# Seven block products in place of eight for the first products of two feed-forward blocks

## The chip, the cores and the metric

The kernel runs on one core of a Trainium2 chip. The metric is device time in microseconds, the median of several runs. TensorE (PE) multiplies, VectorE (DVE) and ScalarE (ACT) do element-wise work, GpSimd (POOL) does a little of it, and SyncE (SP) issues the transfers (DMA) that bring weights from memory. Each engine takes its instructions in the order in which they were written to it.

## What is computed

Two transformer blocks follow each other on 1024 tokens of 1024 features; only their feed-forward parts are touched. Block 1 has 2816 inner features (22 tiles of 128), block 2 has 4096 (32 tiles).

```python
# block 1
h = rms_norm(x, g_ffn) * (1.0 + sc_f) + sh_f
x = x + g_f * ((silu(h @ w_ffn_gate) * (h @ w_ffn_up)) @ w_ffn_down)
# block 2
h = rmsnorm(x, norm_mlp_g)
x = x + square(relu(h @ w_up)) @ w_down
```

## The kernel before

Activations are kept transposed, features on the 128 partitions: x is 8 feature tiles (k) by two token halves (t) of 512 columns. Each fp32 operand is split into a high and a low part: ACT casts the high one, DVE or POOL subtracts it for the low one (`split`, `weights`). Each 128x128 by 128x512 product is then three matmuls: high by high (L253), low activation (L254), low weight (L255). Names ending in h and l are these parts: hh and hl of the normalised input, uh and ul of the inner activation, wh and wl of the weights.

`ffn` (L1144) runs in chunks of inner tiles. For a chunk it first makes the first products (`up`, 8 k-tiles each, gate and up in block 1, up alone in block 2), evacuates each from its PSUM bank (sg is silu of the gate; re is relu, then squared), and splits it into uh and ul (`u_split`). Then come the second products (`down`): for each of 8 output tiles and both token halves the chunk's inner tiles are summed in a bank and added to x by DVE (L100 in block 1, L97 in block 2). Block 1's chunks are 2, 4, 4, 4, 4, 4 inner tiles, block 2's are eight chunks of 4. In a down chunk a group is two output tiles, the first token half ahead of the second; so the last u of a chunk (inner tile 3, second half) is wanted by the 34th matmul of the group, behind 33 others.

PE's order is that of the code. Work that was put off (`later`, `tick`) is written between matmuls: the normalised input of the second token half (`make_h`) is made while the first half is multiplied. Weights are fetched by SP into wr (two buffers of 512 KB), each transfer issued when the buffer's last reader is done. SP also writes x out for a later use (`spill`, x1d). In the last chunk of block 1 `evac_last` also sums the squares of x twice, once on DVE and once on POOL (acc, through buffers ta, four of them).

Of the kernel before, what the change touches and what calls it, by code (L numbers as in the profile page):

```python
# [5 lines left out]
F32 = mybir.dt.float32  # L6
F32R = mybir.dt.float32r
# [6 lines left out]
P = 128  # L14
# [9 lines left out]
HOLD = 1  # L24


TAGS = {
    "g": (32, 512),
    "pt": (6, 512),
    "h": (32, 512),  # L30
    "wr": (2, 1024),
    "wh": (2, 1024),
    "wl": (2, 1024),
    "e": (7, 1024),
    "td": (4, 512),
    "ta": (4, 512),
}


def rev(ap, n):  # L40
# [10 lines left out]
class Build:  # L51
    def __init__(self, tc, a, out, dbg=None):
        self.tc, self.nc, self.a, self.out = tc, tc.nc, a, out
        self.dbg = dbg or {}
        self.n = 0
        self.bg = None
        self.due = {"d": [], "s": []}
        self.dense, self.b, self.ready = None, 0.0, set()
        self.pend = []
        self.pre, self.pace = [], 1  # L60
        self.low = self.nc.gpsimd
        self.fresh = set()
        self.quarter = None


    def nm(self, s):
# [1 line left out]
        return f"{s}_{self.n}"  # L68

    def al(self, tag, dt=F32, cols=None, name=None):  # L70
        bufs, w = TAGS[tag]
        return self.sb.tile([P, cols or min(w, 1024)], dt, name=self.nm(name or tag), tag=tag, bufs=bufs)

    def small(self, cols, tag, bufs=2, dt=F32):
        return self.sb.tile([P, cols], dt, name=self.nm(tag), tag=tag, bufs=bufs)
# [251 lines left out]
        self.nc.scalar.copy(r, ps)  # L327
        return r

    def rstd_then(self, acc, n, eps, then, gap=3):  # L330
        d = self.rtok([acc], n, eps)[0]
        self.later(gap, lambda: then(self.spread(d)))


    def consts(self):
# [748 lines left out]
    def block1_mix(self):  # L1084
        self.gdo = self.const(1, "gdo")
        self.ts(self.gdo, self.v("g_diff_out"), 1.0 - LAM_INIT, ALU.mult)
        self.dn = self.const(64, "dn")
        self.dnd = self.dram([32, P], "dnd")
        self.alibi()
        self.modd = self.dram([4, 2, H], "modd")  # L1090
        self.bg = self.mod_later()
        self.xd = self.spill("xd", 2)
        od = [[self.dram([P, H], "od") for _ in range(2)] for _ in range(8)]
        self.D = {}
        t3, tl = self.t_gemm(24), self.t_gemm(48)
# [36 lines left out]
        def evac2(n, t, ps):  # L1132
            evac(n, t, ps)
            self.sq_acc(accs, t, self.x[n][t])
        self.hh, self.hl = self.h_tiles()

        def done(t):
            def then(r):
                for k in range(KT):
                    self.later(1 + (2 - t) * k, lambda k=k: self.make_h(self.hh, self.hl, k, t, r, A[:, k : k + 1], sh[:, k : k + 1]))  # L1140
            self.rstd_then(accs[t], T, self.eps1, then)
        self.drain(self.gemm(W, 512, 4, cols, hh, hl, evac2, done, gsz=8))

    def ffn(self, chunks, up, down, evac_down, evac_last, done, gsz, cut=False):  # L1144

        c0 = 0
        for ci, c in enumerate(chunks):
            uh, ul = [[None, None] for _ in range(c)], [[None, None] for _ in range(c)]
            self.drain(up(c0, c, uh, ul))
            last = ci == len(chunks) - 1  # L1150
            self.drain(self.gemm(down, c0 * P, c, [[(i * P, P)] for i in range(8)], uh, ul,
                                 evac_last if last else evac_down, done if last else None, gsz=gsz if last else 2, cut=cut))
            c0 += c

    def u_split(self, tmp, uh, ul, i, t):
        tag = "g" if i < 3 else "pt"
        uh[i][t], ul[i][t] = self.al(tag, F32R, name="uh"), self.al(tag, F32R, name="ul")
        self.split(tmp, uh[i][t], ul[i][t])

    def block1_ffn(self):  # L1160
        Wg, Wu = self.a["w_ffn_gate"][0], self.a["w_ffn_up"][0]

        def up(c0, c, uh, ul):
            nt = []
            for i in range(c):
                nt += [(Wg, [((c0 + i) * P, P)]), (Wu, [((c0 + i) * P, P)])]
            hold = {}

            def evac(n, t, ps):
                if n % 2 == 0:  # L1170
                    hold[t] = self.al("td", name="sg")
                    self.act(hold[t], ps, AF.Silu)
                else:
                    s = hold[t]
                    self.tt(s, ps, s, ALU.mult)
                    self.u_split(s, uh, ul, n // 2, t)
            return self.gemm(None, 0, KT, nt, self.hh, self.hl, evac, gsz=2)
        g = self.mod[:, 40:48]
        gf = self.v("g_final", 0, 8)
        gg = self.const(8, "gg")  # L1180
# [6 lines left out]
        def evac_last(n, t, ps):  # L1187
            evac(n, t, ps)
            self.sq_acc(a1, t, self.x[n][t])
            self.sq_acc(a2, t, self.x[n][t], scale=gf[:, n : n + 1], tag="e", eng=self.nc.gpsimd if n < KT - 1 else None)  # L1190
        hh, hl = self.h_tiles()

        self.r1 = self.const(8, "r1")
# [1 line left out]
        def done(t):  # L1195
# [13 lines left out]
            d = v[:, 4:8]  # L1209

            def then():
                r = self.spread(d)
# [339 lines left out]
    def block2_mix(self):  # L1552
# [72 lines left out]
            self.sq_acc(accs, t, self.x[n][t])  # L1625
        self.hh, self.hl = self.h_tiles()

        def done(t):
            def then(r):
                for k in range(KT):  # L1630
                    self.later(1 + (2 - t) * k, lambda k=k: self.make_h(self.hh, self.hl, k, t, r, self.v("norm_mlp_g_2", k), tag="gh"[t]))
            self.rstd_then(accs[t], T, self.eps2, then)
        self.drain(self.gemm(W, 0, KT, cols, hh, hl, evac2, done, gsz=2))

    def block2_ffn(self):
        Wu = self.a["w_up_2"][0]

        def up(c0, c, uh, ul):
            def evac(n, t, ps):
                s = self.al("td", name="re")  # L1640
                self.act(s, ps, AF.Relu)
                self.tt(s, s, s, ALU.mult)
                self.u_split(s, uh, ul, n, t)
            return self.gemm(Wu, 0, KT, [[((c0 + i) * P, P)] for i in range(c)], self.hh, self.hl, evac, gsz=2)
        accs = {}

        def evac(n, t, ps):
# [21 lines left out]
        def done(t, s):  # L1669
# [29 lines left out]
                elif hf:  # L1699
                    self.nc.sync.dma_start(out=d, in_=o)  # L1700
            for i in range(n):
                o = self.al("e", name="out")
# [14 lines left out]
    def run(self, upto=99):  # L1717
        tc = self.tc
        with tc.tile_pool(name="sb", bufs=1) as self.sb, tc.tile_pool(name="ps", bufs=1, space=PSUM) as self.ps, \
                tc.tile_pool(name="dp", bufs=1, space=DRAM) as self.dp:  # L1720
            with tc.manual_schedule(engines={mybir.EngineType.PE}):
                self.phases(upto)

    def phases(self, upto):
        self.block1_in()
# [51 lines left out]
```

## Time and profile before

| what | us |
|---|---|
| median of 3 runs | 3242.78 (3242.65 to 3246.18) |
| profiled execution | 3245.43 |
| its span | 3243.5 |
| PE busy in it | 3109.9 (96%) |
| DVE, ACT, POOL busy | 1792.0, 1250.5, 428.1 |
| block 1 feed-forward, first matmul to last | 655.3 to 1400.5 |
| block 2 feed-forward, first matmul to last output | 2513.2 to 3243.5 |

A matmul of 512 columns is shown with about 0.4 us but the next one starts 0.23 us later: they overlap, so the pace is read from starts. A gap in the starts with "[idle <- engine tile]" is time in which PE waited for that tile.

### The profile page before, as it was taken

What the parts mean: (1) busy time and instruction counts of PE and PEld (TensorE: products, weight loads), DVE (VectorE), ACT (ScalarE), POOL (GpSimd) and SP (SyncE); (2) the same over time, 40 slices, a digit from 0 to 9 for tenths busy, and PEclk for the clock granted to TensorE, in tenths of its full rate; (3) what the DMA queues carried; (4) which work ended last, traced back from release to release, by engine and by line L of the source; (5) the groups of instructions that cost most, each with busy time, mean ns of one, the idle gap of its engine ahead of it and who ended that gap; (6) DMA issues with size and microseconds to landing.
All of it is one profiled execution on the core that took longest, in us unless ns stands there. A gap on an engine that the chain in (4) does not pass through costs nothing. (4 is left out here: it accounts for less than half of the span.)

```text
span 3243.5 us, 39354 instructions
## 1 busy us (share of the span) xinstructions
PE 3109.9 (96%) x15270; PEld 2528.2 (78%) x15270; DVE 1792.0 (55%) x2999; ACT 1250.5 (39%) x2220; POOL 428.1 (13%) x431
## 2 busy tenths in 40 slices
PE   6899999999999999989999998999999999999999
PEld 4777778878888888868777776877788788888888
DVE  5666677552322323367777779778973533333335
ACT  4444576331111111355665664555532322211215
POOL 3101111110000000043332332111112100000000
PEclk8999999999999999999999999999999999999999
DMA  8434304111111111232222221222531111111111
GB/s 266 111 94 115 100 24 146 40 39 46 52 46 46 52 43 48 81 82 62 66 64 60 54 56 34 85 74 77 172 95 46 46 46 46 52 46 46 52 46 72
DMA packets 265036, 229.37 MB, mean 71 GB/s; under 512 B 16908, under 2 KB 221562, under 8 KB 264850
## 3 DMA queue, kind: packets, MB, share of 16 engines
q1 hardware_dynamic: 257408, 214.14, 22.8%
q10 hardware_dynamic: 7090, 12.65, 1.0%
q8 instruction: 120, 1.97, 0.3%
q14 instruction: 66, 0.54, 0.1%
q0 software_dynamic: 352, 0.07, 0.0%
HBM read 176.91 MB, written 24.74 MB: 62 GB/s over the span
## 5 line engine op out<-in xcount | busy, mean ns | idle before, releaser
L253 PE MATMUL mm<-hh,wh 128*128 128x512 f32 (+1 forms) x2208 | 887.3, 402 | 12.3 <-ACT wh L201 7.5
L255 PE MATMUL mm<-hh,wl 128*128 128x512 f32 (+1 forms) x2208 | 879.4, 398 | 1.3 <-POOL wl L202 1.2
L254 PE MATMUL mm<-hl,wh 128*128 128x512 f32 (+1 forms) x2208 | 873.4, 396 | 2.5 <-DVE hl L97 2.4
L201 ACT CAST wh<-wr 128x1024 fp32r<-128x1024 f32 (+3 forms) x231 | 231.2, 1001 | 810.7 <-PE mm L254 657.6
L253 PEld LDWEIGHTS mm<-hh,wh 128*128 128x128 f32 (+1 forms) x2208 | 415.5, 188 | 103.8 <-ACT wh L201 7.7
L255 PEld LDWEIGHTS mm<-hh,wl 128*128 128x128 f32 (+1 forms) x2208 | 414.8, 188 | 103.6 <-POOL wl L202 2.5
L254 PEld LDWEIGHTS mm<-hl,wh 128*128 128x128 f32 (+1 forms) x2208 | 415.3, 188 | 94.6 <-DVE hl L97 3.0
L202 POOL TENSOR_TENSOR wl<-wr,wh 128x1024 fp32r<-128x1024 f32 (+3 forms) x105 | 234.5, 2235 | 1046.2 <-ACT wh L201 962.4
L254 PE MATMUL mm<-ul,wh 128*128 128x512 f32 (+1 forms) x816 | 316.7, 388 | 0.0
L253 PE MATMUL mm<-uh,wh 128*128 128x512 f32 (+1 forms) x816 | 316.4, 388 | 0.0
L255 PE MATMUL mm<-uh,wl 128*128 128x512 f32 (+1 forms) x816 | 316.0, 387 | 0.0
L202 DVE TENSOR_TENSOR wl<-wr,wh 128x1024 fp32r<-128x1024 f32 (+1 forms) x126 | 152.3, 1208 | 207.3 <-ACT wh L201 202.6
L97 DVE TENSOR_TENSOR x<-x,mm 128x512 f32<-128x512 f32 (+1 forms) x168 | 111.0, 661 | 239.0 <-PE mm L255 238.1
L1285 DVE TENSOR_TENSOR_SCAN u<-u 128x128 f32<-128x128 f32 (+7 forms) x128 | 177.8, 1389 | 76.6 <-POOL u L1281 76.1
L253 PEld LDWEIGHTS mm<-uh,wh 128*128 128x128 f32 x816 | 153.3, 188 | 33.2
L254 PEld LDWEIGHTS mm<-ul,wh 128*128 128x128 f32 x816 | 153.2, 188 | 32.9
L255 PEld LDWEIGHTS mm<-uh,wl 128*128 128x128 f32 x816 | 153.1, 188 | 32.2
L97 DVE TENSOR_TENSOR sg<-mm,sg 128x512 f32<-128x512 f32 x43 | 29.7, 691 | 258.2 <-PE mm L255 258.2
L100 DVE SCALAR_TENSOR_TENSOR x<-mm,mod,x 128x512 f32<-128x512 f32 x128 | 95.5, 748 | 132.4 <-PE mm L255 131.9
L108 ACT ACTIVATE u<-sc 128x512 f32<-128x512 f32 (+2 forms) x192 | 95.0, 495 | 96.2 <-PE sc L1273 94.6
L108 ACT ACTIVATE p<-p,mx 128x128 f32<-128x128 f32 (+7 forms) x96 | 74.6, 778 | 105.0 <-DVE mx L97 67.5
L97 DVE TENSOR_TENSOR al<-tp,ah 128x512 fp32r<-128x512 f32 (+1 forms) x160 | 99.3, 621 | 23.1 <-ACT ah L112 22.9
(392 smaller groups left out, 5037.2 us busy)
## 6 DMA issues: line engine op xcount, KB each, us to landing
wr<-in_w_in SPq DMA_DIRECT2D x65, 512.0 KB
wada<-in_w_ada SPq DMA_DIRECT2D x48, 512.0 KB
wr<-in_w_up SPq DMA_DIRECT2D x32, 512.0 KB
wr<-in_w_down SPq DMA_DIRECT2D x32, 512.0 KB
wr<-in_w_out SPq DMA_DIRECT2D x24, 512.0 KB
wr<-in_w_ffn_gate SPq DMA_DIRECT2D x22, 512.0 KB
wr<-in_w_ffn_up SPq DMA_DIRECT2D x22, 512.0 KB
wr<-in_w_ffn_down SPq DMA_DIRECT2D x20, 512.0 KB
```

Source lines behind the costliest of these rows:

```text
L97: return self.nc.vector.tensor_tensor(o, i0, i1, op)
L100: return self.nc.vector.scalar_tensor_tensor(o, i0, s, i1, op0, op1)
L108: return self.nc.scalar.activation(o, i, f, **k)
L201: self.nc.scalar.copy(wh[:, :n], raw[:, :n])
L202: (low or self.low).tensor_tensor(wl[:, :n], raw[:, :n], wh[:, :n].bitcast(F32), ALU.subtract)
L253: mm(o, lhsT=wh[:, k, :], rhs=xh[k][t][:, s], start=(k == 0), stop=False)
L254: mm(o, lhsT=wh[:, k, :], rhs=xl[k][t][:, s], start=False, stop=False)
L255: mm(o, lhsT=wl[:, k, :], rhs=xh[k][t][:, s], start=False, stop=(k == KC - 1))
L1285: nc.vector.tensor_tensor_scan(ur, ur, ur, 1.0, ALU.mult, ALU.bypass)
```

## The change

The first products of every chunk but the first are made in groups (`pair_weights`, `pair_job`) of two output tiles by two token halves, with the eight k-tiles in two halves of four: a 2x2 by 2x2 block product with seven block products (P1 to P7) in place of eight. Each block product is 4 k-tiles of three matmuls, 12 in all. In block 1 a group is the gate and the up of one inner tile (20 groups), in block 2 two inner tiles (15 groups). The sums of activation blocks (T: P5, P6, P7, P4) are made once at each feed-forward's start by `make_t` (y0, t2, t3, t4, split into th and tl); the sums of weight blocks are made by DVE for each group (P6, P7, P3; buffers ws). Every block product has its own 128x512 weight split in a buffer wc, of which there are four; the two halves of a chunk's down weights take two 128x1024 wc each. Three banks collect: U (P1, P6, P7, P4), A (P2), V (P5, P3); ACT copies a partial sum out (c), DVE adds them, and `fin` does the silu or relu and the split.

Chunks are two inner tiles (11 in block 1, 16 in block 2). Down tiles run first half, second half, output tile by output tile, 6 matmuls each. Chunk 0 is made plainly (`first_chunk`). Job i's fetch is written seven jobs ahead and its weights two jobs ahead. Buffers are laid out anew (`layout`): MIX outside, FFN inside the feed-forward parts, with four wr, four wc, eight u and two ta.

```diff
+ORDER = ("P1", "P2", "P6", "P5", "P7", "P3", "P4")
+BANK = {"P1": "U", "P2": "A", "P6": "U", "P5": "V", "P7": "U", "P3": "V", "P4": "U"}
+FFN = {"td": (4, 512), "ta": (2, 512), "wr": (4, 1024), "ws": (2, 1024), "wc": (4, 1024), "u": (8, 512), "hx": (8, 512)}
...
+        def sums(k):
+            q = k + 4
+            y0 = self.al("td", name="y0")
+            self.stt(y0, self.x[k][0], col(A, k), r[0], ALU.mult, ALU.mult)
+            t2 = self.al("td", name="t2")
+            self.tt(y0, y[k], y0, ALU.subtract)
+            plus(t2, y[q], sh is None or col(sh, q), y0)
+            pair("P5", k, y0)
...
+        self.t_work = [lambda k=k: sums(k) for k in range(4)] + [lambda k=k: last(k) for k in range(4)]
+        for k in range(early):
+            self.later(9 + 2 * k, lambda: self.t_work.pop(0)())
...
+        def make(p):
+            if p == "P6":
+                s = self.al("ws")
+                st["s"] = (s[:, :H], s[:, H:])
+                self.tt(st["s"][0], side(1, 0), side(1, 1), ALU.add)
+                self.tt(st["s"][1], st["s"][0], side(0, 0), ALU.subtract)
+            elif p == "P7":
+                self.tt(side(1, 0), side(0, 0), side(1, 0), ALU.subtract)
+            elif p == "P3":
+                self.tt(st["s"][1], side(0, 1), st["s"][1], ALU.subtract)
...
+            w = self.al("wc", F32R)
+            self.split(src, w[:, :H], w[:, H:])
...
+        for k, (xh, xl) in enumerate(self.moving(p)):
+
+            mm(o, lhsT=wh[:, k, :], rhs=xh, start=(new and k == 0), stop=False, skip_group_check=True)
+            mm(o, lhsT=wh[:, k, :], rhs=xl, start=False, stop=False, skip_group_check=True)
+            mm(o, lhsT=wl[:, k, :], rhs=xh, start=False, stop=(k == 3), skip_group_check=True)
+            self.tick()
+        if p in ("P1", "P6", "P5"):
+            st["c" + p] = self.al("td", name="c")
+            self.nc.scalar.copy(st["c" + p], o)
+        elif p == "P2":
+            self.tt(st["cP1"], o, st["cP1"], ALU.add)
+            fin(0, 0, st["cP1"])
...
+        else:
+            fin(1, 0, o)
...
+        def make():
+            hi, lo = self.al("wc", F32R), self.al("wc", F32R)
+            self.split(st["raw"], hi, lo)
...
+                        for n in range(4 * g, 4 * g + 4):
+                            for t in range(2):
+                                self.down_tile(st, n, t, (), uh, ul, evac_down)
...
+        self.first_chunk([s for two in pairs(0) for s in two], plain(0))
+        self.flush()
+        while self.t_work:
+            self.t_work.pop(0)()
+        fetched = made = 0
+        for i in range(len(jobs)):
+            while fetched < min(len(jobs), i + 8):
+                if jobs[fetched][0]:
+                    jobs[fetched][0]()
+                fetched += 1
+            while made < min(len(jobs), i + 3):
+                jobs[made][1]()
+                made += 1
+            jobs[i][2]()
...
-        self.ffn([2, 4, 4, 4, 4, 4], up, self.a["w_ffn_down"][0], evac, evac_last, done, 8)
+        self.ffn(11, pairs, plain, fin, self.a["w_ffn_down"][0], evac, evac_last, done)
+        self.layout(MIX)
...
-        self.ffn([4] * 8, up, self.a["w_down_2"][0], evac, evac_last, done, 8, cut=True)
+        self.ffn(16, pairs, plain, fin, self.a["w_down_2"][0], evac, evac_last, done, cut=True)
```

DVE at the end of a chunk's first products in block 1, before (sg and ul of the last two inner activations, wl the low parts of the coming down weights, x the first down tile's evacuation):

```order
L97 TENSOR_TENSOR ul_8058<-sg_8029,uh_8057 128x512
L202 TENSOR_TENSOR wl_8121<-wr_8118,wh_8120 128x1024
L97 TENSOR_TENSOR sg_8086<-mm_8088,sg_8086 128x512
L202 TENSOR_TENSOR wl_8183<-wr_8180,wh_8182 128x1024
L97 TENSOR_TENSOR ul_8115<-sg_8086,uh_8114 128x512
L100 SCALAR_TENSOR_TENSOR x_5341<-mm_8124,mod,x_5341 128x512
```

The same place after the change (c_8428 the second token half's silu and product, wc_8489 the low part of the down weights' second half, c_8386 the product of P4's bank mm_8373, ul_8506 its split, x_5344 the first down tile's evacuation):

```order
L106 TENSOR_TENSOR wr_8410<-wr_8408,wr_8410 128x512
L106 TENSOR_TENSOR c_8428<-tp_8434,c_8428 128x512
L106 TENSOR_TENSOR c_8428<-c_8447,c_8428 128x512
L106 TENSOR_TENSOR wc_8489<-wr_8388,wc_8488 128x1024
L106 TENSOR_TENSOR ul_8485<-c_8428,uh_8484 128x512
L106 TENSOR_TENSOR c_8386<-mm_8373,c_8386 128x512
L106 TENSOR_TENSOR ul_8506<-c_8386,uh_8505 128x512
L109 SCALAR_TENSOR_TENSOR x_5344<-mm_8512,mod,x_5344 128x512
```

The 128x1024 low part, which stood among evacuations that had a chunk's matmuls before their use, now stands between the last two activations; its buffer is the one that P4's weights leave, and the product of P4 and its split stand behind it.

DVE at the first down chunk of block 2, before (re and ul are inner activations, wl the low part of a weight, x_19951 the first down tile's evacuation):

```order
L97 TENSOR_TENSOR re_21740<-re_21740 128x512
L97 TENSOR_TENSOR ul_21744<-re_21740,uh_21743 128x512
L202 TENSOR_TENSOR wl_21814<-wr_21811,wh_21813 128x1024
L97 TENSOR_TENSOR re_21772<-re_21772 128x512
L97 TENSOR_TENSOR ul_21776<-re_21772,uh_21775 128x512
L202 TENSOR_TENSOR wl_21876<-wr_21873,wh_21875 128x1024
L97 TENSOR_TENSOR re_21804<-re_21804 128x512
L97 TENSOR_TENSOR x_19951<-x_19951,mm_21817 128x512
```

The same place after (y, t and tl are sums of `make_t` and their low parts, wc_22301 and wc_22305 the low parts of the first down weights):

```order
L106 TENSOR_TENSOR tl_22261<-y_4714_22255,th_22260 128x512
L106 TENSOR_TENSOR t_4697_22162<-t_4697_22162,t_4715_22257 128x512
L106 TENSOR_TENSOR tl_22267<-t_4715_22257,th_22266 128x512
L106 TENSOR_TENSOR t_4720_22270<-y_22082,y_22073 128x512
L106 TENSOR_TENSOR tl_22281<-t_4675_22100,th_22280 128x512
L106 TENSOR_TENSOR wc_22301<-wr_22292,wc_22300 128x1024
L106 TENSOR_TENSOR tl_22273<-t_4720_22270,th_22272 128x512
L106 TENSOR_TENSOR tl_22285<-t_4697_22162,th_22284 128x512
L106 TENSOR_TENSOR wc_22305<-wr_22294,wc_22304 128x1024
L106 TENSOR_TENSOR tl_22289<-t_4697_22162,th_22288 128x512
L106 TENSOR_TENSOR x_20462<-x_20462,mm_22311 128x512
```

The sums of `make_t` now stand in DVE's row ahead of the first down weights' low part and of the first evacuation.

SP at the end of block 1, before (x1d are spills, in_w_in the weights of block 2's first product):

```order
L194 DMA wr_10392<-in_w_ffn_down 128x4x256
L194 DMA wr_10867<-in_w_in 128x8x128
L515 DMA x1d_10787<-x_5341 128x512
L515 DMA x1d_10789<-x_5343 128x512
L194 DMA wr_10873<-in_w_in 128x8x128
L515 DMA x1d_10791<-x_5345 128x512
```

The same place after:

```order
L524 DMA x1d_11277<-x_5368 128x512
L524 DMA x1d_11279<-x_5370 128x512
L524 DMA x1d_11281<-x_5372 128x512
L524 DMA x1d_11283<-x_5374 128x512
L203 DMA wr_11348<-in_w_in 128x8x128
L203 DMA wr_11354<-in_w_in 128x8x128
L203 DMA wr_11602<-in_w_in 128x8x128
```

The first two weight transfers, which stood ahead of and among the spills, now stand behind all sixteen.

## Rows read from the trace of the kernel before

**Rows 1.** The page, busy time by engine, then TensorE and its clock by slice.

```profile
PE 3109.9 (96%) x15270; PEld 2528.2 (78%) x15270; DVE 1792.0 (55%) x2999; ACT 1250.5 (39%) x2220; POOL 428.1 (13%) x431
...
PE   6899999999999999989999998999999999999999
...
PEclk8999999999999999999999999999999999999999
```

**Rows 2.** Busy time by stretch: window, length, PE, PEld, DVE, ACT, POOL, clock, DMA.

```profile
655.30:704.90 49.60, 47.74 (x209) 37.65 (x210) 22.35 (x29) 19.57 (x32) 7.52 (x6) 1.00 0.05 17
...
816.30:860.30 44.00, 44.00 (x194) 35.96 (x193) 17.45 (x21) 4.72 (x6) 0.00 (x0) 1.00 0.16 48
860.30:950.00 89.70, 89.70 (x386) 72.17 (x385) 19.97 (x23) 17.02 (x24) 0.00 (x0) 1.00 0.16 47
...
2513.20:2543.40 30.20, 26.21 (x114) 19.28 (x113) 25.83 (x30) 14.69 (x26) 15.26 (x9) 1.00 0.07 21
...
2565.50:2609.70 44.20, 44.20 (x195) 36.12 (x194) 16.47 (x22) 5.44 (x7) 0.00 (x0) 1.00 0.17 48
2609.70:2654.10 44.40, 44.40 (x194) 36.20 (x193) 14.96 (x19) 12.57 (x19) 0.00 (x0) 1.00 0.15 48
...
3183.60:3243.50 59.90, 54.15 (x369) 49.48 (x367) 33.34 (x61) 35.60 (x64) 0.00 (x0) 0.97 0.21 80
```

**Rows 3.** Timeline of PE at the end of a block 1 down chunk: start, length, instruction.

```profile
993.70 0.40 PE L255 MATMUL mm<-uh,wl 128*128 128x512 f32 x1
993.93 0.40 PE L253 MATMUL mm<-hh,wh 128*128 128x512 f32 x1
```

**Rows 4.** DVE instructions by line, block 1, 860.3 to 1350: count, busy, mean ns.

```profile
L202 DVE TENSOR_TENSOR wl<-wr,wh 128x1024 fp32r<-128x1024 f32 x44 | 53.9, 1226 | 73.2 <-ACT wh L201 69.9
L100 DVE SCALAR_TENSOR_TENSOR x<-mm,mod,x 128x512 f32<-128x512 f32 x49 | 36.8, 750 | 80.3 <-PE mm L255 80.1
L97 DVE TENSOR_TENSOR sg<-mm,sg 128x512 f32<-128x512 f32 x31 | 21.4, 692 | 192.5 <-PE mm L255 192.5
L97 DVE TENSOR_TENSOR ul<-sg,uh 128x512 fp32r<-128x512 f32 x31 | 21.3, 688 | 11.0 <-ACT uh L112 11.0
```

**Rows 5.** ACT instructions by line, same stretch.

```profile
L112 ACT CAST uh<-sg 128x512 fp32r<-128x512 f32 x31 | 19.2, 621 | 92.7 <-DVE sg L97 92.7
```

**Rows 6.** Timeline of PE at two idle gaps and behind them.

```profile
1403.27 0.47 PE L253 MATMUL mm<-hh,wh 128*128 128x512 f32 x1 [2.77 <-DVE x L100]
...
1404.05 0.63 PE L253 MATMUL mm<-hh,wh 128*128 128x512 f32 x1
1404.48 0.63 PE L254 MATMUL mm<-hl,wh 128*128 128x512 f32 x1
...
2517.89 0.50 PE L254 MATMUL mm<-hl,wh 128*128 128x512 f32 x1 [2.36 <-DVE hl L97]
2518.23 0.39 PE L255 MATMUL mm<-hh,wl 128*128 128x512 f32 x1
2518.46 0.40 PE L253 MATMUL mm<-hh,wh 128*128 128x512 f32 x1
```

**Rows 7.** Timeline of DVE, first rows of the second token half, block 2.

```profile
2525.77 2.08 DVE L100 SCALAR_TENSOR_TENSOR xn<-x,vec,r 128x512 f32<-128x512 f32 x3 [1.29 <-ACT r L327]
```

**Rows 8.** Timeline of SP around block 1's end: weight and spill issues.

```profile
1355.33 0.37 SPq L194 DMA_DIRECT2D wr<-in_w_in  x1
1356.60 1.19 SPq L515 DMA_DIRECT2D x1d<-x  x2
1359.51 0.38 SPq L194 DMA_DIRECT2D wr<-in_w_in  x1
```

**Rows 9.** SP: a gate weight issued ahead of block 1's feed-forward.

```profile
641.20 0.37 SPq L194 DMA_DIRECT2D wr<-in_w_ffn_gate  x1
```

**Rows 10.** POOL and ACT by line in block 1's last chunk, 1350.9 to 1400.5.

```profile
L302 POOL TENSOR_TENSOR acc<-acc,sq 128x512 f32<-128x512 f32 x10 | 14.0, 1402 | 691.7 <-ACT sq L108 690.2 <-DVE acc L302 1.5
...
L108 ACT ACTIVATE sq<-x,vec 128x512 f32<-128x512 f32 x11 | 7.8, 712 | 0.0
```

More of the change, by code (lines that the diff above doesn't have):

```diff
@@ L63, in __init__ @@
         self.quarter = None
+        self.rest = None
     def nm(self, s):
@@ L328, in spread, with rstd_then @@
         return r
-    def rstd_then(self, acc, n, eps, then, gap=3):
+    def rstd_then(self, acc, n, eps, then, gap=3, tag="ta"):
         d = self.rtok([acc], n, eps)[0]
-        self.later(gap, lambda: then(self.spread(d)))
+        self.later(gap, lambda: then(self.spread(d, self.al(tag, name="r"))))
     def consts(self):
@@ L1141, in done @@
-            self.rstd_then(accs[t], T, self.eps1, then)
+                    self.later(1 + 2 * k, lambda k=k: self.make_h(self.hh, self.hl, k, t, rt, A[:, k : k + 1], sh[:, k : k + 1]))
+            self.rstd_then(accs[t], T, self.eps1, then, tag="g")
         self.drain(self.gemm(W, 512, 4, cols, hh, hl, evac2, done, gsz=8))
[L1144 to L1153, printed above, removed]
@@ new lines, in pair_job @@
+    def pair_job(self, st, p, fin):
+        mm = self.nc.tensor.matmul
+        bank = BANK[p]
+        new = p in ("P1", "P2", "P5")
+        if new:
+            st[bank] = {"U": self.mm, "A": self.sc, "V": self.tp}[bank]()
+        o = st[bank]
+        wh, wl = st[p]
+        for k, (xh, xl) in enumerate(self.moving(p)):
[9 more added lines that the diff above has]
+            fin(0, 0, st["cP1"])
+        elif p == "P7":
+            self.tt(st["cP5"], o, st["cP5"], ALU.add)
+            fin(1, 1, st["cP5"])
+        elif p == "P3":
+            self.tt(st["cP6"], o, st["cP6"], ALU.add)
+            fin(0, 1, st["cP6"])
+        else:
+            fin(1, 0, o)
@@ new lines, in down_tile @@
+    def down_tile(self, st, n, t, c, uh, ul, evac):
+        mm = self.nc.tensor.matmul
+        ps = self.mm()
+        s = c[0] if c else slice(0, H)
+        wh, wl = st["w"]
+        d = slice((n % 4) * P, (n % 4) * P + P)
+        for k in range(2):
+            o = ps[:, s]
+            mm(o, lhsT=wh[:, k, d], rhs=uh[k][t][:, s], start=(k == 0), stop=False)
+            mm(o, lhsT=wh[:, k, d], rhs=ul[k][t][:, s], start=False, stop=False)
+            mm(o, lhsT=wl[:, k, d], rhs=uh[k][t][:, s], start=False, stop=(k == 1))
+            self.tick()
+        evac(n, t, ps, *c)
@@ new lines, in first_chunk @@
+    def first_chunk(self, srcs, evac):
+        mm = self.nc.tensor.matmul
+        n, w = len(srcs), []
+        for i, (W, c0) in enumerate(srcs):
+            raw = self.al("wr")
+            self.nc.sync.dma_start(out=raw.rearrange("p (k n) -> p k n", k=KT), in_=W[:, c0 : c0 + P].rearrange("(k p) n -> p k n", p=P))
+            parts = []
+            for f in range(2):
+                if i < 2:
+                    x = self.al("wc", F32R)
+                    parts.append((x[:, :H], x[:, H:]))
+                else:
+                    parts.append([self.al("g", F32R, name="w") for _ in range(2)])
+                self.split(raw[:, f * H : f * H + H], *parts[-1])
+            w.append([[x.rearrange("p (k n) -> p k n", k=4) for x in two] for two in parts])
+        for t in range(2):
+            if self.hh[7][t] is None:
+                while self.hh[7][t] is None:
+                    self.tick()
+            order = [(i, k) for i in range(n) for k in ((0, 4, 1, 5, 2, 6, 3, 7) if t else range(KT))]
+            if t:
+                at = {k: j for j, k in enumerate((0, 4, 1, 5, 2, 6, 3, 7))}
+                order.sort(key=lambda x: (x[0] // 2, at[x[1]] + LAG * (x[0] % 2)))
+            else:
+                order.sort(key=lambda x: (x[0] // 2, x[1] + LAG * (x[0] % 2)))
+            ps, seen = {}, {}
+            for i, k in order:
+                if i not in ps:
+                    ps[i] = self.sc() if t else self.mm()
+                    seen[i] = 0
+                wh, wl = (x[:, k % 4, :] for x in w[i][k // 4])
+                xh, xl = self.hh[k][t], self.hl[k][t]
+                mm(ps[i], lhsT=wh, rhs=xh, start=(seen[i] == 0), stop=False)
+                mm(ps[i], lhsT=wh, rhs=xl, start=False, stop=False)
+                mm(ps[i], lhsT=wl, rhs=xh, start=False, stop=(seen[i] == KT - 1))
+                seen[i] += 1
+                if seen[i] == KT:
+                    evac(i, t, ps[i])
+                self.tick()
@@ L1161, in block1_ffn, with pairs, plain @@
         Wg, Wu = self.a["w_ffn_gate"][0], self.a["w_ffn_up"][0]
[L1163 to L1166, printed above, removed]
+        self.layout(FFN)
+        def pairs(c):
+            return [((Wg, (2 * c + i) * P), (Wu, (2 * c + i) * P)) for i in range(2)]
+        def plain(c):
             hold = {}
@@ L1636, in block2_ffn, with pairs, take, plain @@
         Wu = self.a["w_up_2"][0]
[L1638 to L1644, printed above, removed]
+        self.layout(FFN)
+        def pairs(c):
+            return [((Wu, 2 * c * P), (Wu, (2 * c + 1) * P))]
+        def take(c, n, t, x, s):
+            self.act(s, x, AF.Relu)
+            self.tt(s, s, s, ALU.mult)
+            self.u_split(s, c, n, t)
+        def plain(c):
+            return lambda n, t, ps: take(c, n, t, ps, self.al("td", name="re"))
+        def fin(c, i):
+            return lambda n, t, x: take(c, n, t, x, self.al("td", name="re") if (n, t) == (1, 0) else x)
         accs = {}
```

175 lines of the change are left out of this document (146 added, 29 removed).

## The prediction

> **What bounds the kernel now.** The page comes first. TensorE is busy 96% of the span and in nearly every slice at full clock; no other engine passes 55% [rows 1]. Inside the feed-forward parts it is busier still: in an up chunk and a down chunk of block 1, and in both kinds of block 2, busy time equals the window while VectorE is busy for 40% at most and GpSimd not at all [rows 2]. The timeline shows the last down matmul of a chunk and the first up matmul of the next 0.23 us apart [rows 3]: there is no wait at a chunk's end. So here the count of matmuls is the time: 384 in 89.7 us are 0.2336 us each, 192 in 44.4 us are 0.2312 [rows 2]. What the change takes out counts in full; what it makes TensorE wait for counts in full too.
>
> **What is taken out.** Chunk 0 stays plain. Block 1 keeps 20 groups of 96 products, block 2 15; each loses one block product of 12. That is 240 x 0.2336 = 56 us and 180 x 0.2312 = 42 us, together **-98 us**. Down matmuls stay as many.
>
> **The groups themselves.** A group has 84 matmuls, 19.5 us. In it VectorE has about 17 rows of 0.6 to 0.7 us [rows 4], 11 us, and ScalarE some 8.5 us. Both fit, and each bank's add or copy stands one block product (2.8 us) ahead of its next use. I cost these at nothing, covered by the 19.5 us; were the weight transfer that VectorE's sums wait for a microsecond later than this cover, each of the 35 groups would lose it.
>
> **The wait at a chunk's end** is new, ten times in block 1 and fifteen in block 2. The first down tile of the first half takes the u of P4 with its fourth matmul. In VectorE's row ahead of that u stand the low part of the second half's down weights and the low part of another u. The first waits for P4's last matmul, whose buffer wc it takes. From there: 0.17 us until the last product is there (shown length 0.40 against a pace of 0.23, rows 3), 1.15 for the 128x1024 low part, 0.61 for the ul, 0.69 for the product, 0.62 for ScalarE's cast, 0.69 for its low part [rows 4, 5]; back to back rows start 0.08 us before the last one's end (three rows of 0.75 take 2.08, rows 7), so the first two are shortened by it. That is 3.93 us, less the four matmuls that can run (0.94), plus some 0.2 for four changes of engine: 3.2 us. In block 2 the product is preceded by ScalarE's relu and VectorE arrives a little late from the weight sums: 3.2 to 3.6, I take 3.4. The lower end, if neither of the two foreign rows were ahead, is 3.2 - 1.76 = 1.4 us. Before, the same u had 33 matmuls (7.7 us) of cover. 10 x 3.2 + 15 x 3.4 = **+83 us**.
>
> **The clock.** After an idle gap of 2.77 us TensorE ran at 1.2 GHz for a stretch: starts 0.43 us apart [rows 6]. After one of 2.36 us they stayed 0.23 apart, at 2.4 GHz [rows 6]. The slow stretch at 1400 has eight matmuls of which the rows show two; each costs 0.196 us more, 1.57 in all. The new gaps of about 2.6 us plus 0.5 behind one matmul lie between and above these two. I take a fall in two of three, 16 of 25: **+25 us**; the ends are 0 and 39. The Trainium skill (TensorE: Matmul & The Clock Gate, HAM oscillation) gives idle time per gap at which the clock is lost, and these gaps stay below its figure. By that rule no chunk end would cost clock and the sum would be 25 lower; the row after 2.77 us speaks against it, so it is a rival only.
>
> **Entry of block 1.** Before, its weights were issued from 641.2 on, 14 us ahead of the first matmul at 655.3 [rows 9, 2]. Now they wait for the last sum of squares of the mixer, since the new layout lies over its buffers; with 4 to 5 us from issue to use TensorE idles some 7 us, and the second half's statistics stand behind the eight weight splits for another 2. Before, the same 192 matmuls took 49.6 us for 44.9 [rows 2], so the net is +4 to 5. Then the remaining sums of `make_t` stand among the first down evacuations: about 30 rows of 0.65 us where the first four tiles need 5.5 us, some 11 us of waits, after which the clock may fall. Together 15 to 21, I take **+18**.
>
> **Exit of block 1.** The last chunk has 6 matmuls per output tile and half, 1.4 us, where before it had 12. Its squares go through two buffers in place of four: ScalarE's square 0.71 and GpSimd's add 1.40 [rows 10] follow each other, 2.1 per tile. For 14 tiles that is +9, some of it absorbed. Also the first weights of the next product, issued at 1355.3 and 1359.5 among the spills [rows 8], now stand behind the last spill, which waits for the last evacuation; their cast and low part come then: +4. **+13**.
>
> **Entry of block 2.** Before, the first 96 products took 30.2 us for 22 [rows 2]. Now the second half's statistics come ahead of all of them (some 6 us after the mixer's last matmul), and from there VectorE has about 9 rows, then 61 more up to the low part of the first down weights: 15 at 0.67, 45 at 0.61, one at 1.15 [rows 4, 7], 39 us. TensorE has 96 matmuls, 22 us. So the first down tile starts some 50 us after the mixer where it could before at 30. With a fall of the clock **+22**. The end below, if VectorE's rows overlap with work ahead of the statistics, is +10.
>
> **Tail.** Output tiles again have half the matmuls per evacuation, and the last window already took 59.9 us [rows 2]: 0 to 6, I take **+3**.
>
> Sum: -98 + 83 + 25 + 18 + 13 + 22 + 3 = **+66**. The profiled execution took 3245.4 us, 2.6 above the median; 3242.8 + 66 = **3309 us**.
>
> **Rivals.** (1) The same waits, but the clock holds at the chunk ends and entries: 3309 - 25 - 6 = **3278**. For it: the gap of 2.36 us that cost no clock. Against: the row after 2.77. (2) Faster: the chunk-end wait is the short one. If VectorE does P4's product before the foreign rows bind (by being ready when P4 ends, the weights' buffer coming free sooner than I read), it is 1.4 us; 25 x 1.4 = 35, no clock lost, and the rest at its lower ends (15 + 13 + 10 + 0 = 38): -98 + 35 + 38 = -25, **3218**. With the rest at these ends and no falls it decides at 60 / 25 = 2.4 us per chunk end: below that the change gains. Against: the row order of VectorE as written. (3) All waits are hidden and the 98 us arrive: **3145**; nothing in the rows of VectorE's order supports it. (4) The weight transfers come late in each group: 35 x 1 us more, **3344**. For it: transfers are issued only when a split has freed one of four buffers; against: two block products of slack.
>
> **How the numbers follow.** The forecast has 0.52, rival 1 0.22, rival 2 0.13, rival 3 0.03, rival 4 0.10. About 0.2% (6.5 us) is what a measurement of this kernel can tell from no change. Rival 2's spread (3210 to 3245) gives 0.11 to faster and 0.02 to no change; rival 1's lower end adds 0.04 to no change and 0.01 to faster. So faster 0.15, same 0.06, slower 0.79. The range from 3245 to 3350 leaves out rivals 2 and 3 and a little of rival 4.
>
> **What would show it.** In the profile of the changed kernel: TensorE's matmuls 420 fewer in these parts; at each chunk end an idle gap of about 2.6 us ended by ScalarE's cast uh and a smaller one ended by ul, with VectorE's 128x1024 low part right behind P4's end; slow starts of 0.43 us behind many of them; an idle stretch of 10 us or more ahead of block 2's first down tile, ended by the low part of its weights; a group of 84 matmuls in 19.5 us. The prediction is wrong if chunk ends show gaps under 2 us, if groups take more than 20.5 us, or if the entries' gaps are missing.

## The result, and the profile after

The changed kernel takes 3330.81 us (3328.65 to 3332.72, four runs); the kernel before took 3244.48 us beside it (3242.65 to 3246.72, four runs). The ratio is 1.0266, with a 95% interval of 1.0248 to 1.0283. The forecast was 3309 us, range 3245 to 3350: the side and the range were right, the size 22 us short. The profiled execution has a span of 3326.9 us where before it was 3243.5, so 83.4 us are to be found.

The page first, to be read beside [rows 1]: busy time by engine, then TensorE and its clock by slice.

```profile
PE 3072.0 (92%) x14802; PEld 2494.1 (75%) x14802; DVE 2205.6 (66%) x3724; ACT 1393.4 (42%) x2532; POOL 405.5 (12%) x419
...
PE   6999999899999999889999999999997999999998
...
PEclk8999999999999999999999999999998999999999
```

TensorE has fewer instructions and is busy for 38 us less, but for 92% of the span in place of 96%. VectorE's work grew from 1792 to 2206 us. Where TensorE waits is in the view of its waits (waiting tile and line, what it waited for; total, times, longest). First comes the first of the three down matmuls (L1309) on ScalarE's cast uh, 26 times. Of the five rows quoted the kernel before has in its feed-forward only the fourth kind, the wait for x, with 1.6 us:

```profile
PE mm L1309 <- ACT uh L121: 73.5, 26, 3.3
...
PE mm L262 <- ACT wh L210: 17.9, 2, 10.9
PE mm L1311 <- DVE wc L106: 14.3, 1, 14.3
PE mm L1309 <- DVE x L109: 9.0, 6, 3.8
PE mm L1348 <- ACT wc L121: 8.1, 1, 8.1
```

They are, from the top, the chunk ends (25 of the 26 waits; one lies in the entry of block 2), the exit of block 1 (the 10.9; the other 6.9 us lie outside the feed-forward), the entry of block 2, and the last two mostly the entry of block 1. Busy time by stretch shows the chunks, as in [rows 2]: two groups of block 1, a down chunk there, a down chunk of block 2 and a group there.

```profile
741.70:780.40 38.70, 38.70 (x169) 31.58 (x168) 19.88 (x30) 15.94 (x26) 0.00 (x0) 1.00 0.22 66
780.40:805.50 25.10, 22.34 (x98) 17.96 (x97) 17.47 (x25) 2.38 (x4) 0.00 (x0) 1.00 0.09 25
2711.90:2740.00 28.10, 25.09 (x98) 19.83 (x98) 15.33 (x23) 2.98 (x5) 0.00 (x0) 0.88 0.06 21
2739.90:2759.40 19.50, 19.50 (x86) 15.85 (x85) 11.75 (x18) 9.60 (x15) 0.00 (x0) 1.00 0.26 74
```

The groups are full: busy equals the window. The two down chunks hold the same 96 matmuls and take 25.1 and 28.1 us (others of block 1 26.2 to 27.8); at the pace before (half of 44.0 or 44.2 in [rows 2]) they would take 22.0 to 22.1. The granted clock beside them is 1.00 and 0.88.

Where the 83.4 us come from, by taking the same marker (the end of a mixer, the first matmul of a chunk) in both traces, to rounding:

| part | after minus before, us | forecast |
|---|---|---|
| first mixer (not touched) | -4.5 | 0 |
| entry of block 1, to the end of its first down tiles | +19.7 | +18 |
| eight steady chunks of block 1, 65.16 for 66.83 | -13.4 | -11.2 |
| the last two chunks and the exit of block 1 | +13.4 | +10.2 |
| second mixer (not touched) | -4.4 | 0 |
| entry of block 2 | +24.9 | +22 |
| 14 steady chunks of block 2, 47.49 for 44.16 | +46.7 | +22.8 |
| tail, with block 2's last chunk | +1.2 | +4.6 |

(The forecast's chunks are its terms put together: in block 1 24 matmuls fewer, 3.2 of wait and 25 / 25 = 1.0 of clock, -1.4 each; in block 2 12 fewer, 3.4 and 1.0, +1.6. The exit is 13 less two chunks, the tail 3 and one chunk.) Block 2's chunks are the miss.

**A chunk end.** Timeline of TensorE in block 1, then in block 2, as in [rows 3]:

```profile
780.87 0.40 PE L1311 MATMUL mm<-uh,wc 128*128 128x512 f32 x1
783.80 0.50 PE L1309 MATMUL mm<-uh,wc 128*128 128x512 f32 x1 [2.54 <-ACT uh L121]
784.53 0.50 PE L1310 MATMUL mm<-ul,wc 128*128 128x512 f32 x1 [0.23 <-DVE ul L106]
784.86 0.39 PE L1311 MATMUL mm<-uh,wc 128*128 128x512 f32 x1
...
2759.91 0.40 PE L1311 MATMUL mm<-uh,wc 128*128 128x512 f32 x1
2763.37 0.80 PE L1309 MATMUL mm<-uh,wc 128*128 128x512 f32 x1 [3.06 <-ACT uh L121]
2764.09 0.80 PE L1310 MATMUL mm<-ul,wc 128*128 128x512 f32 x1
2764.69 0.63 PE L1311 MATMUL mm<-uh,wc 128*128 128x512 f32 x1
2765.11 0.63 PE L1309 MATMUL mm<-uh,wc 128*128 128x512 f32 x1
...
2769.38 0.50 PE L1310 MATMUL mm<-ul,wc 128*128 128x512 f32 x1
```

Three matmuls run (the row at 780.87 is the third) and the fourth waits for the last activation. Starts 2.93 and 0.73 us apart in place of 0.23 make a wait of 3.2 us; 3.46 and 0.72 in block 2 make 3.7. Behind the second gap starts are 0.60 and then 0.43 apart until 2769.38, eleven of them by 0.43: that is 1.2 GHz. Behind the first they are 0.33 and then 0.23 apart, 2.4 GHz at once. VectorE at the first of the two:

```profile
780.68 1.22 DVE L106 TENSOR_TENSOR wc<-wr,wc 128x1024 fp32r<-128x1024 f32 x1
781.81 0.68 DVE L106 TENSOR_TENSOR ul<-c,uh 128x512 fp32r<-128x512 f32 x1
782.41 0.68 DVE L106 TENSOR_TENSOR c<-mm,c 128x512 f32<-128x512 f32 x1
783.78 0.69 DVE L106 TENSOR_TENSOR ul<-c,uh 128x512 fp32r<-128x512 f32 x1 [0.68 <-ACT uh L121]
```

P4's last matmul starts at 780.18 and ends some 0.4 later. Then come the two foreign rows, the product of P4 at 782.41, ScalarE's cast, and ul: the order of the forecast.

### The profile page after: what moved, and what is told of

Its sections match the earlier page's. It is cut to its first block, busy times and chain, and to the rows that moved or that the text cites. A ratio compares the mean times of both kernels' runs of the same rounds, so it can differ in the third digit from the quotient of the medians.

```text
span 3326.9 us, 39496 instructions
## 1 busy us (share of the span) xinstructions
PE 3072.0 (92%) x14802; PEld 2494.1 (75%) x14802; DVE 2205.6 (66%) x3724; ACT 1393.4 (42%) x2532; POOL 405.5 (12%) x419
## 5 line engine op out<-in xcount | busy, mean ns | idle before, releaser
L1309 PE MATMUL mm<-uh,wc 128*128 128x512 f32 (+1 forms) x880 | 371.1, 422 | 82.4 <-ACT uh L121 73.5
L262 PE MATMUL mm<-hh,wh 128*128 128x512 f32 (+1 forms) x1024 | 420.5, 411 | 18.2 <-ACT wh L210 17.9
L264 PE MATMUL mm<-hh,wl 128*128 128x512 f32 (+1 forms) x1024 | 408.7, 399 | 4.0 <-POOL wl L211 4.0
L263 PE MATMUL mm<-hl,wh 128*128 128x512 f32 (+1 forms) x1024 | 405.2, 396 | 0.0
L1311 PE MATMUL mm<-uh,wc 128*128 128x512 f32 (+1 forms) x880 | 361.3, 411 | 14.3 <-DVE wc L106 14.3
L1310 PE MATMUL mm<-ul,wc 128*128 128x512 f32 (+1 forms) x880 | 368.1, 418 | 2.5 <-DVE ul L106 2.3
L1309 PEld LDWEIGHTS mm<-uh,wc 128*128 128x128 f32 x880 | 179.9, 204 | 134.2 <-ACT uh L121 84.8
L262 PEld LDWEIGHTS mm<-hh,wh 128*128 128x128 f32 (+1 forms) x1024 | 193.2, 189 | 54.5 <-ACT wh L210 18.5
L264 PEld LDWEIGHTS mm<-hh,wl 128*128 128x128 f32 (+1 forms) x1024 | 192.3, 188 | 53.4 <-POOL wl L211 6.5
L1311 PEld LDWEIGHTS mm<-uh,wc 128*128 128x128 f32 x880 | 180.4, 205 | 52.2 <-DVE wc L106 14.8
L263 PEld LDWEIGHTS mm<-hl,wh 128*128 128x128 f32 (+1 forms) x1024 | 193.4, 189 | 34.2
L1267 PE MATMUL mm<-th,wc 128*128 128x512 f32 x420 | 165.4, 394 | 0.0
L1269 PE MATMUL mm<-th,wc 128*128 128x512 f32 x420 | 164.9, 393 | 0.0
```

Of the source, the lines that this page charges most:

```text
L262: mm(o, lhsT=wh[:, k, :], rhs=xh[k][t][:, s], start=(k == 0), stop=False)
L263: mm(o, lhsT=wh[:, k, :], rhs=xl[k][t][:, s], start=False, stop=False)
L264: mm(o, lhsT=wl[:, k, :], rhs=xh[k][t][:, s], start=False, stop=(k == KC - 1))
L1267: mm(o, lhsT=wh[:, k, :], rhs=xh, start=(new and k == 0), stop=False, skip_group_check=True)
L1269: mm(o, lhsT=wl[:, k, :], rhs=xh, start=False, stop=(k == 3), skip_group_check=True)
L1309: mm(o, lhsT=wh[:, k, d], rhs=uh[k][t][:, s], start=(k == 0), stop=False)
```

## The experiments

My theory: the chunk ends cost (a) a wait made by two rows of VectorE that stand ahead of P4's product, and (b) the clock that falls behind the wait. Its rivals: chunks of two tiles cost of themselves, or the new pools of buffers do. For the entry and the exit the question was whether the place of one row makes the gap, a queue, or plain work. Ratios are to the kernel before, run beside each on its chip. In the recorded texts e1 is the run with five weight buffers, e2 the one with the half order too, e6 that with the spills on ScalarE, e7 that with the first down weights ahead of the sums.

**Five weight buffers.** With a fifth wc the low part no longer waits for P4's last matmul. The two ta of the feed-forward pool pay for it; the squares of the last chunks, which went through them, now go through the four td.

```diff
-FFN = {"td": (4, 512), "ta": (2, 512), "wr": (4, 1024), "ws": (2, 1024), "wc": (4, 1024), "u": (8, 512), "hx": (8, 512)}
+FFN = {"td": (4, 512), "wr": (4, 1024), "ws": (2, 1024), "wc": (5, 1024), "u": (8, 512), "hx": (8, 512)}
```

> The changed kernel with five wc buffers in place of four (the two ta buffers give their room; squares of the last chunks go through td). The low part of the second half's down weights then takes the buffer that P3 leaves, 2.8 us ahead of P4's end, and stands ahead of P4's end in VectorE's row. Theory (the foreign 128x1024 row between P4's end and its u makes most of the wait, and the wait makes the slow clock): the wait at a chunk's end falls from 3.2 us (block 1) and 3.7 us (block 2) to about 1.9, so -13 -27 us; starts of 0.43 us at the chunk ends go from some 200 to nearly none, -40 us; four td in place of two ta shorten block 1's exit by up to 8. Together about 3243 us. Rival (the chain product, cast, low part of P4 itself sets the wait): waits and slow starts stay, 3322 to 3331 us.

Measured: 3254.20 us, ratio 1.0020 (1.0010 to 1.0029): 77 us of the loss are gone. In the traces 67 us come off in the 23 steady down chunks; 4 come off in block 1's last down chunk and exit, which the squares' four buffers may have a part in, and 2 in block 2's last down chunk. VectorE and TensorE at a chunk end of block 1, then TensorE at one of block 2:

```profile
843.34 1.21 DVE L106 TENSOR_TENSOR wc<-wr,wc 128x1024 fp32r<-128x1024 f32 x1
844.47 0.68 DVE L106 TENSOR_TENSOR c<-c,c 128x512 f32<-128x512 f32 x1
845.48 0.69 DVE L106 TENSOR_TENSOR c<-mm,c 128x512 f32<-128x512 f32 x1 [0.32 <-PE mm L1269]
...
846.90 0.50 PE L1309 MATMUL mm<-uh,wc 128*128 128x512 f32 x1 [0.76 <-ACT uh L121]
848.03 0.49 PE L1310 MATMUL mm<-ul,wc 128*128 128x512 f32 x1 [0.63 <-DVE ul L106]
...
2730.01 0.50 PE L1309 MATMUL mm<-uh,wc 128*128 128x512 f32 x1 [1.53 <-ACT uh L121]
2731.00 0.80 PE L1310 MATMUL mm<-ul,wc 128*128 128x512 f32 x1 [0.49 <-DVE ul L106]
2731.60 0.63 PE L1311 MATMUL mm<-uh,wc 128*128 128x512 f32 x1
```

The low part now runs under P4, and the product starts when P4 is done. The wait is 1.8 us in block 1, with no slow start, and 2.5 in block 2, where 5 of 14 chunk ends still lost clock for 6 or 7 matmuls; the five are every third end, 133 us apart. (a) holds. The rest to the expected time are these falls and block 2's longer wait.

**Half order too.** On top of that the down tiles take the second token half first, whose last activation is not P4's; in block 2, where it comes late as well, its inner tiles are taken in the other order.

```diff
-        for k in range(2):
+        ks = (1, 0) if t and late == 2 else (0, 1)
+        for k in ks:
...
-                            for t in range(2):
+                            for t in (1, 0) if c else (0, 1):
```

> As e1, and in the down chunks the second token half's tile comes ahead of the first's, in block 2 with its inner tile from P7 ahead of that from P3: P4's u is wanted by the 11th matmul in place of the 5th. Theory: the wait at a chunk's end falls to about 0.6 us, no slow starts: e1 less another 1.3 x 25 = 32 us, about 3211 us, below the kernel before. Rival (another wait, the matmul pace or the entries set the time): no gain over e1.

Measured: 3220.83 us, ratio 0.9918 (0.9903 to 0.9933). This is 0.8% faster than the kernel before. Every steady down chunk takes 22.5 us in block 1 and 23.2 in block 2, with no slow start; the waits are 0.6 and 1.25 us.

**The order alone**, with four wc, to see whether one of the two did it all.

> The changed kernel with only the order of the down tiles of e2 (second half first), four wc buffers as in the changed kernel. Theory: VectorE's row is as in the changed kernel (low part of the down weights, ul, product, ul behind P4's end, 3.9 us), but the second half's u is the first wanted and P4's only with the 11th matmul: the two waits together are 1.4 to 2.0 us a chunk's end in place of 3.2 and 3.7, slow starts mostly gone: 25 x 1.7 + 40 = 82 less than the changed kernel, about 3248 us. Rival (the fifth buffer is what counts, the order adds little): 3300 us or more.

Measured: 3259.21 us (3251.13 to 3265.10, three runs), ratio 1.0032 (1.0013 to 1.0051). Waits are 1.9 to 2.5 us, in three pieces, and hardly a start is slow. The order by itself takes off some 72 us, the buffer some 77, both 110. Of that the 23 steady down chunks give 71, 67 and 104 us in the traces: each shortens the same wait, and each is mostly enough to keep the clock.

**The gap filled.** The changed kernel, its order and waits left alone, with ten matmuls whose result nobody uses behind the third down matmul. The edit reaches the 23 steady chunks, not 24 as the text below says.

```diff
+            if warm and k == 0:
+                pv = self.pv()
+                for _ in range(warm):
+                    mm(pv, lhsT=wh[:, 0, d], rhs=uh[0][t], start=True, stop=True)
```

> The changed kernel with ten matmuls of 512 columns into an unused bank written behind the third matmul of the 24 down chunks behind a group (not block 1's or block 2's last); their result is not used. They run in the gap of 2.6 us and take 2.3 us of it. Theory (the idle gap is what lets the clock fall to 1.2 GHz): the gaps stay as long in all, slow starts there vanish, about 40 us less: 3290 us. Rival (the slow starts have another cause, or cost nothing that is not waited for anyway): 3325 to 3335 us.

Measured: 3285.78 us (two runs), ratio 1.0120 (1.0096 to 1.0144). TensorE at a chunk end of block 2, and the down chunk's window:

```profile
2746.91 0.40 PE L1311 MATMUL mm<-uh,wc 128*128 128x512 f32 x1
2747.14 2.46 PE L1315 MATMUL pv<-uh,wc 128*128 128x512 f32 x10
2750.39 0.50 PE L1309 MATMUL mm<-uh,wc 128*128 128x512 f32 x1 [0.79 <-ACT uh L121]
2751.12 0.50 PE L1310 MATMUL mm<-ul,wc 128*128 128x512 f32 x1 [0.22 <-DVE ul L106]
2751.46 0.40 PE L1311 MATMUL mm<-uh,wc 128*128 128x512 f32 x1
...
2746.40:2772.10 25.70, 24.68 (x107) 19.81 (x107) 15.40 (x23) 2.98 (x5) 0.00 (x0) 1.00 0.08 25
```

The fourth matmul comes 3.48 us after the third, as late as without the fillers (3.46), so the wait is untouched. But starts behind it are 0.23 apart, the window's clock is 1.00, and the chunk takes 25.7 us for 28.2. The difference of the two medians, 45 us, is therefore what falls of the clock cost at the chunk ends: (b), measured by itself. The chunks' lengths in the two traces give 44.

**Chunks of two alone.** The kernel before, with `[2] * 11` and `[2] * 16` as its chunks.

> The kernel before with chunks of two inner tiles in both blocks and all eight products, its own buffers and its own order of down tiles. Theory (the smaller chunk alone costs little; the waits come from the seven products' rows and buffers): 3243 to 3257 us, the excess in the last chunks, no gaps at chunk ends. Rival (smaller chunks make the chunk ends wait by themselves): 25 more or less equal gaps, 3280 us or more.

Measured: 3247.69 us, ratio 1.0001 (0.9992 to 1.0011). Chunk ends there have no gap: the last of a chunk's first products starts at 772.95, the down matmuls behind it at 773.18, 773.42, 773.65 and 773.88, where the changed kernel waits ahead of its fourth. The smaller chunk by itself is not the cause; it only doubles the number of places where the new wait falls.

**The pools alone.** The kernel before, with KEEP and MIX as two pools. It was to explain the 9 us that the untouched mixers gained.

> The kernel before with its buffers in the two pools of the changed kernel (g and h ahead, the rest behind in the order of the changed kernel), chunks, products and every engine's order as before. In the changed kernel the two mixers, which the change does not touch, took 4.5 and 4.4 us less, with matmul starts some 2 ns closer. Theory (where the operands lie sets the pace of matmuls): the mixers' matmuls start 0.230 to 0.232 us apart as in the changed kernel, about 9 us less: 3236 us. Rival (something else in the changed kernel made the mixers faster): 0.232 to 0.234 us and 3245 us as before.

Measured: 3241.96 us, ratio 0.9975 (0.9963 to 0.9988). The theory fell: the pace of the second mixer's 128x512 matmuls (mean of the starts less than 0.26 us apart) is 233.5 ns, as before (233.0), where the changed kernel and those derived from it have 230.2. The kernel is a little faster all the same, though its profiled execution of 3244.74 us does not show where.

**The spills on another queue.** On the faster kernel (five buffers and half order), to bring back the exit: the last writes of x are issued by ScalarE in place of SyncE, so that the next weights don't stand behind them.

```diff
-                    self.nc.sync.dma_start(out=d[k][t], in_=x[k][t])
+                    (self.nc.sync if gap else self.nc.scalar).dma_start(out=d[k][t], in_=x[k][t])
```

> As e2, with the sixteen spills of x at block 1's end issued by ScalarE in place of SyncE, so that the weights of block 2's first product stand first on SyncE. There the changed kernel idles 11.3 us between block 1's last down matmul and the next product, e2 11.7 us. Theory (the weights' transfers stand behind the spills): the gap falls to 3 to 6 us, 6 to 8 us less than e2, about 3214 us. Rival (the gap is the statistics and the casts, not the weights): no change from e2, 3221 us.

Measured: 3217.13 us, ratio 0.9900 (0.9887 to 0.9914), and the gap of the exit is as long as it was. What the traces show of the gain lies ahead of the gap: from the last product of block 1's last group to the last down matmul it is 31.1 us, where e2 had 33.8. ScalarE ahead of it, issues and work, and TensorE:

```profile
1369.37 3.77 ACTq L524 DMA_DIRECT2D x1d<-x  x6
1373.18 1.99 ACT L210 CAST wh<-wr 128x1024 fp32r<-128x1024 f32 x2 [3.42 <-DMA x1d<-x]
...
1374.28 0.80 PE L262 MATMUL mm<-hh,wh 128*128 128x512 f32 x1 [11.70 <-ACT wh L210]
```

The cast now stands behind ScalarE's own issues. So I tried GpSimd as their issuer, which issues no weights and makes no cast. (That run has the next edit too, which lies elsewhere.)

> As e7, with the sixteen spills issued by GpSimd in place of ScalarE: the weights of block 2's first product are first on SyncE, and their casts have no spill ahead of them in ScalarE's row (in e6 and e7 six spills in one stretch of 3.8 us stood right ahead of the cast that ended the gap of 11.7 us). Theory (weights and spills together make block 1's exit gap): the gap falls from 12 us to 3 to 6, 6 to 9 us less than e7, about 3208 us. Rival (the statistics of the last evacuation set it, or GpSimd's issues delay the sums of squares): no change or more, 3215 to 3222 us.

Measured: 3221.56 us, ratio 0.9918 (0.9903 to 0.9933). The gap stays. The run is also 6 us slower than e7, which differs in the spills alone: from the last product of block 1's last group to the last down matmul it is 36.2 us for 29.9, with GpSimd's issues standing between its sums of squares, as the rival said. SyncE, ScalarE and TensorE (line numbers are this kernel's):

```profile
1325.11 0.99 SPq L206 DMA_DIRECT2D wr<-in_w_in  x2
...
1378.94 0.62 ACT L122 CAST hh<-xn 128x512 fp32r<-128x512 f32 x1 [1.06 <-DVE xn L110]
1379.46 1.04 ACT L213 CAST wh<-wr 128x1024 fp32r<-128x1024 f32 x1
...
1380.56 0.80 PE L265 MATMUL mm<-hh,wh 128*128 128x512 f32 x1 [12.37 <-ACT wh L213]
```

The weights were issued 54 us ahead, and their cast starts without a wait of its own, right behind a cast hh that waited for VectorE: they were there. My theory that the transfer makes the gap fell. What ends the gap is the cast, and it stands behind hh in ScalarE's row. That its place makes the whole gap is not shown: the product needs all eight hh of the first token half, and the last of them is cast only behind it, at 1381.28.

**First down weights ahead of the sums.** The entry of block 2: the first eight fetches and two sets of weights are written before the remaining sums of `make_t`.

```diff
+        fetched = made = 0
+        while fetched < 8:
...
+        while made < 2:
+            jobs[made][1]()
+            made += 1
         while self.t_work:
             self.t_work.pop(0)()
-        fetched = made = 0
```

> As e6, with the first chunk's down weights written ahead of the remaining sums of make_t, so that their low parts stand earlier in VectorE's row. Theory (VectorE's rows ahead of the first down tile are more than TensorE's work there; it is the bound at both entries): the gap of 15.1 us at block 2's first down tile becomes shorter, but the first evacuation still stands behind the sums, so the wait moves to the fourth tile (three banks): 2 to 6 us less than e6 in all. Rival (only the place of that row costs the 15 us): 12 us or more less than e6.

Measured: 3215.32 us, ratio 0.9896 (0.9883 to 0.9910), the fastest of all here, but by less than the runs can tell from the one it was built on. The first down chunk takes 40.4 us; without the edit it took 40.2. TensorE's two longest gaps in it:

```profile
2524.23 0.80 PE L1310 MATMUL mm<-uh,wc 128*128 128x512 f32 x1 [3.47 <-ACT uh L121]
...
2536.88 0.80 PE L1310 MATMUL mm<-uh,wc 128*128 128x512 f32 x1 [6.13 <-DVE x L106]
```

Gaps of 14.3, 2.6 and 0.7 us became six that add up to 14.2, and the chunk is as long as it was. VectorE is busy for 33.3 us of its 40.4. So the place of this one row is not what costs; that VectorE's work there is the bound fits these numbers, but no run here had less of it.

**Block 1 alone.** The version just told, with block 2's feed-forward as in the kernel before.

> As e7 in block 1, with block 2's feed-forward as in the kernel before (eight products, chunks of four, its own buffers). Theory (in block 2 even the mended groups give back at the entry what they save: in e7 block 2 takes 734.2 us from the mixer's last matmul to the end, in the kernel before 730.5): 0 to 6 us less than e7, 3210 to 3215 us. Rival (the seven products pay in block 2 too): 3222 us or more.

Measured: 3218.94 us, ratio 0.9914 (0.9897 to 0.9931). That is between the theory's range and the rival's. So even mended, block 2's seven products bring nothing that these runs can show: its chunks save some 1.5 us each, and the entry takes 25.

## Why the prediction was right, and by how much it was off

**The matmuls.** 56 + 42 = 98 us were to go. A group has 84 matmuls in 19.46 us in block 2, as forecast; block 1's two take 38.70, a pace of 0.230 where before it was 0.234, so its 20 groups save 61 and not 56. Sum -103. No group waited (rival 4 is out).

**The wait at a chunk's end** was forecast at 3.2 and 3.4 us; it is 3.2 and 3.7, so 10 x 3.2 + 15 x 3.7 = 88 us for 83. The rows of VectorE are those of the forecast, and taking away what one of them waited for took the wait with it (without it 1.8 and 2.5 are left, where rival 2 had 1.4).

**The clock is the term that was mis-sized.** I took a fall in 16 of 25 ends, eight matmuls each, 25 us, with 39 as the upper end. In the trace 21 of the 23 steady ends fell. Block 1's have 4 to 12 slow starts, 48 in all over nine ends; of block 2's 14 one has none, one 7 and the others 11 or 12, 147 in all. At 0.196 us more each that is 38 us, and 19 starts 0.36 late ahead of the slow stretch add 7: 45 us, as the filled gap measured. The ends of the two last chunks, with five slow starts each, add 3. Both choices were too small, the share and the length. The eight matmuls came from one stretch of [rows 6], and they were misread: it has six, starting from 1404.05 to 1406.18, and the next wait cuts it off. I had compared a gap's length with two rows, 2.77 and 2.36 us, but the length of one gap does not decide: 2.54 us at 783.80 cost nothing, nor did 3.18 at 2624.14, the third longest of the 23, and the fifth buffer's 1.53 and 0.49 fell in five of 14 ends and stayed in the others, alike in every row ahead of them. Rival 1, that the clock holds, is out. The rule of the Trainium skill (TensorE: Matmul & The Clock Gate, HAM oscillation), by which gaps as short as these keep the clock, would have left the sum 45 us short; the measurement decides against it here.

**Entry of block 1**, 18 forecast, 19.7 measured. The idle of 7 us is 8.1, on the cast of the first weights, and the first down tiles wait for their evacuations behind the sums (2.3, 3.8 and 1.5 us):

```profile
658.18 0.80 PE L1348 MATMUL mm<-hh,wc 128*128 128x512 f32 x1 [8.11 <-ACT wc L121]
...
714.27 0.50 PE L1309 MATMUL mm<-uh,wc 128*128 128x512 f32 x1 [2.29 <-DVE x L109]
720.59 0.80 PE L1309 MATMUL mm<-uh,wc 128*128 128x512 f32 x1 [3.79 <-DVE x L109]
725.04 0.80 PE L1309 MATMUL mm<-uh,wc 128*128 128x512 f32 x1 [1.52 <-DVE x L109]
```

**Exit of block 1**, 13 forecast, about 17 measured, and the cause of its second half was wrong. The evacuations of the last chunk cost some 7 us for 9. The rest, 9.5 us for 4, was to be weights issued behind the spills [rows 8]. The changed kernel's gap, with ScalarE's row ahead of it (the weights were issued at 1407.98, 8 us before their cast):

```profile
1415.44 0.62 ACT L121 CAST hh<-xn 128x512 fp32r<-128x512 f32 x1 [1.06 <-DVE xn L109]
1415.97 1.04 ACT L210 CAST wh<-wr 128x1024 fp32r<-128x1024 f32 x1
...
1417.06 0.80 PE L262 MATMUL mm<-hh,wh 128*128 128x512 f32 x1 [10.94 <-ACT wh L210]
```

The weights' cast has no idle ahead of it, and the run with the spills on GpSimd's queue kept the gap although its weights were issued 54 us ahead. In the kernel before, the same casts ran at 1380.45 and 1388.69, well ahead of the last down matmul at 1400.11. I read the queue that changed and not the row that follows it. That the cast moved behind hh is read from two traces; no run here put it back, so what that would give stays open.

**Entry of block 2**, 22 forecast, 24.9 measured. The longest gap has the low part of the down weights behind VectorE's sums, as forecast. TensorE, then VectorE:

```profile
2576.88 0.80 PE L1311 MATMUL mm<-uh,wc 128*128 128x512 f32 x1 [14.31 <-DVE wc L106]
...
2575.02 0.67 DVE L106 TENSOR_TENSOR tl<-t,th 128x512 fp32r<-128x512 f32 x1
2575.62 1.21 DVE L106 TENSOR_TENSOR wc<-wr,wc 128x1024 fp32r<-128x1024 f32 x1
```

**The tail** cost nothing, for 3: its row of 1.2 us holds block 2's last chunk, whose wait and slow starts cost 1.7 us more than its group saves. **What I did not foresee** are the mixers, 9 us faster with the same instructions. It hid a part of the miss: without it the time would have been some 31 us over the forecast. Its cause is open; the pools were tried and are not it.

Together: -103 + 88 + 48 + 20 + 17 + 25 - 1 - 9 = +85 us, where the trace has 83.4.

## What to carry to other kernels

Before work is taken off an engine that is busy all the time, list the rows that stand in the helping engine's order between its last result and the first use of it: here two rows that belonged to something else, 1.8 us of them, made about half of a wait of 3.2 to 3.7 us at 25 places, and with the clock behind it and the entries and the exit a gain of 100 us became a loss of 86. Count such a gap with the clock it costs behind it; half as much again is what this kernel paid. And free what the foreign row waits for, or write the consumer whose operand is ready first: a fifth buffer and another order of the down tiles were worth 110 us.

## What the runs showed of the hardware that was not expected

- Ten matmuls without a use in waits of 3.2 and 3.7 us kept TensorE at 2.4 GHz at all 23 steady chunk ends, and were worth 45 us. In this kernel work for nothing is better than waiting.
- Gaps alike in length and place lost the clock at some chunk ends and not at others (two of 23 ends in the changed kernel, 9 of 14 in block 2 with five buffers, kept it), and the slow stretch had 4 to 12 matmuls.
- The pace of the same matmul, 128x512 with its weight load, differed between kernels with no wait between: 0.230 to 0.234 us. On 14,800 matmuls a hundredth of that is 34 us, more than some of the terms that I worked out.
